# A hybrid decoder layer: first weights of down's second group split and stored during up, a cast moved behind bank copies, activation halves in two pieces

## The chip, the cores and the metric

The kernel runs on one core of a Trainium2 chip. The time is the device time of one execution in microseconds; before the change its median over three runs is 1188.48 us (1188.13 to 1190.49).

## The reference

One layer for 1024 prompt tokens and 64 decode tokens together (1088 columns), model width 1024, all in float32. A normalised input goes through one input projection into two mixers (retention with 8 heads, and sliding-window attention with 8 query heads), an output projection and a residual. Then comes the part of this case:

```python
hf = rms_norm(h, norm_ffn_gain)
h = h + jnp.square(jax.nn.relu(hf @ w_up)) @ w_down    # w_up: 1024 x 4096, w_down: 4096 x 1024
```

## The kernel before

Float32 products are made of three matmuls: each operand is split into a high half (a cast to float32r on ScalarE) and a low half (the operand minus the high half, on VectorE), and `mm3` multiplies high by high, low by high and high by low. `halve` (lines 791 and 792) is that cast and that subtraction. `wsplit` does it for one 128x512 piece of weights, in a buffer `wa` or `wb` of which there are four each.

Both big products of the MLP use Strassen's scheme with seven products of sums of quarter matrices. `left` is a generator that loads the raw weights of one tile (two loads of 512 KB, on ScalarE's DMA queue), forms the sums on GpSimd (POOL, lines 1046) and yields the split weights product by product. The order of the products is `PROD` for up and `DOWN = (1, 6, 7, 4, 5, 3, 2)` for down. Product one of a tile takes the quarter `a11` itself, the first 512 columns of the raw tile.

Up has 16 tiles, the calls `up(fp)`, of some 21 us each. A tile's squared activations, and their sums for Strassen's right side, are stored to DRAM (`u_d`) in four stores on SyncE's queue, three quarters first (line 1153) and four sums later (line 1173). After up, the pools of its operands are closed and `dn` takes their space.

Down has five groups of tiles: 2, 4, 4, 4 and 2 files of `w_down` (group index `g` = 0 to 4; files 0-1, 2-5, 6-9, 10-13, 14-15). For each group the seven products run in the order of `DOWN`. A product has eight units, (m, s) with m below 4 and s below 2; a unit accumulates over the group's files into one PSUM bank, three matmuls of 128x272 for each file. There are eight banks. Products 1, 5 and 2 start new sums, the others add on to what stands in the banks. After each unit the bank goes to an accumulator `a` in SBUF: the first time by a copy on ScalarE (line 1264, the last one of a product is kept in `copied[i]`), later by an addition on VectorE (line 1267). So a bank is not written by the next product before its copy or addition is done. The activations of a product are loaded from `u_d` (line 1246; for the first group's products seven, four and five at line 1221) and halved into `uh` and `ul`, two files at a time.

The order on each engine is set by a scheduler that simulates the program when it is built. `tc.issue_after(ins)` adds by hand that what is issued inside it on `ins`'s own engine stands behind `ins` in that engine's queue; other engines are not held. For the first product of groups 1 and 2 such ties hold ScalarE's weight loads (and casts) behind copies of the first group:

```python
behind = copied[(6, 6, 7, 4)[f] if g == 1 else 4] if g in (1, 2) and i == 1 else None
with tc.issue_after(behind) if behind else ExitStack():
    ws.append(next(gen))
```

Of the kernel before, what the change touches and what calls it, by code (L numbers as in the profile page):

```python
# [11 lines left out]
F32 = mybir.dt.float32  # L12
F32R = mybir.dt.float32r
AF = mybir.ActivationFunctionType
ALU = mybir.AluOpType
# [5 lines left out]
P = 128  # L21
# [15 lines left out]
def hymba_layer(ctx: ExitStack, tc: tile.TileContext, a: dict, o: dict):  # L37
    nc = tc.nc
# [10 lines left out]
    scratch = ctx.enter_context(tc.tile_pool(name="scratch", bufs=1, space=DRAM))  # L49
# [79 lines left out]
    ms_hi_d = scratch.tile([P, 4, T], F32, name="ms_hi_d")  # L129
    ms_lo_d = scratch.tile([P, 4, T], F32, name="ms_lo_d")  # L130
    y_d = scratch.tile([P, 4, 4, 2, Q], F32, name="y_d")
    u_d = [scratch.tile([P, 2, 2, 7, Q], F32, name=f"u_d{g}") for g in range(8)]

    def rsqrt_inplace(ap, n):
# [171 lines left out]
    w = wload(a["w_in"][2], 8, "wkv", "v")  # L306
    for t in range(9):
        off, c, r0 = tok_tile(t)
# [200 lines left out]
    for blk in range(4):  # L509
        w = wload(a["w_in"][3 + blk], 8, f"wqk{blk}")  # L510
# [9 lines left out]
    for blk in range(2):  # L520
        w = wload(a["w_in"][7 + blk], 8, f"wg{blk}")
# [264 lines left out]
    def pool(name, bufs=1, side=None, space=None):  # L786
        kw = {"space": space} if space else {}
        return tc.tile_pool(name=name, bufs=bufs, side=side, reuse_waits="tile", **kw)

    def halve(hi, lo, src, lo_eng):  # L790
        nc.scalar.copy(hi, src)  # L791
        lo_eng.tensor_tensor(lo, src, hi.bitcast(F32), ALU.subtract)  # L792

    def wsplit(src, tag, name, lo_eng):
        w = (mid if tag == "wb" else mw).tile([P, 2, 512], F32R, tag=tag, name=name, bufs=4)
        halve(w[:, 0, :], w[:, 1, :], src, lo_eng)
        return w
# [170 lines left out]
    mw = ctx.enter_context(pool("mw", side="right"))  # L968
# [54 lines left out]
    opx = ExitStack()  # L1023
# [9 lines left out]
                for x in "hl"  # L1033
            ]

    def left(order, src, name, lo_eng, raw_tag="raw", raw_pool=None, s_tag="S", s_pool=None, tags=("wa", "wb"), raws=None, sums=None):

        r1, r2 = raws or (
            rawload(src[:, i * 1024 : i * 1024 + 1024], f"{name}_r{i + 1}", raw_tag, raw_pool) for i in range(2)
        )  # L1040
        a11, a12, a21, a22 = r1[:, :512], r1[:, 512:], r2[:, :512], r2[:, 512:]
        have = {1: a11, 2: a12, 4: a22, **(sums or {})}

        def comb(i, p_, q_, op):
            t_ = have[i] = (s_pool or mid).tile([P, 512], F32, tag=s_tag, name=f"{name}_s{i}", bufs=10 if s_tag == "Sb" else 4)
            nc.gpsimd.tensor_tensor(t_, p_, q_, op)

        for n, i in enumerate(order):
            if i in (5, 6) and 5 not in have:
                comb(5, a21, a22, ALU.add)  # L1050
                comb(6, have[5], a11, ALU.subtract)
            if i == 7:
                comb(7, a11, a21, ALU.subtract)
            if i == 3:
                comb(3, a12, have[6], ALU.subtract)
            yield wsplit(have[i], tags[n % len(tags)], f"{name}_w{i}", lo_eng)

    late = lambda: bank("pso")
# [9 lines left out]
    for ms in ((0, 1), (2, 3), (4, 5), (6, 7)):  # L1068
# [3 lines left out]
        if ms == (6, 7):  # L1072
# [6 lines left out]
                sums={5: s56[:, :512], 6: s56[:, 512:]})  # L1079
# [13 lines left out]
    ux = ExitStack()  # L1093
    um = ux.enter_context(pool("u", side="right"))

    last_sub = {}

    def up(fp):
        gen = chain(ready, gen0) if fp == 0 else left(
            PROD, a["w_up"][fp], f"wu{fp}", nc.vector, tags=("wa", "wa", "wb", "wb"))  # L1100
        x, y, z = ([bank(f"ps{n}{s}") for s in range(2)] for n in "xyz")
        home = {1: (x, True), 2: (y, True), 6: (x, False), 5: (z, True), 7: (x, False), 4: (x, False), 3: (z, False)}
        ra, rb = ([um.tile([P, n, Q], F32, tag=f"r{n}{s}", name=f"r{n}t{fp}_{s}") for s in range(2)] for n in (3, 4))
        held, wait, ws = {}, [], {}
        order = [(i, s) for i in PROD for s in range(2)]
        if fp == 0:

            order = [(1, 0), (1, 1), (2, 0), (6, 0), (5, 0)] + [(i, 1) for i in (2, 6, 5)] + order[8:]

        def tq(n, s):  # L1110
            return um.tile([P, Q], F32, tag="tq", name=f"{n}{fp}_{s}", bufs=9)

        def add(n, s, bank_):
            t_ = held[n, s]
            nc.vector.tensor_tensor(t_, t_, bank_, ALU.add)
            return t_

        def act(t_, src, s, h, dst):

            nc.vector.scalar_tensor_tensor(t_, src, 0.0, rsf[:, s, h, :], ALU.max, ALU.mult)  # L1120
            return nc.scalar.activation(dst, t_, AF.Square)

        for i, s in order:
            if i not in ws:
                behind = last_sub[0, 0] if (fp, i) in ((1, 3), (2, 6)) else None
                with tc.issue_after(behind) if behind else ExitStack():
                    ws[i] = next(gen)
            w = ws[i]
            bk, first = home[i][0][s], home[i][1]
            for k in range(4):  # L1130
                lh, ll = (w[:, j, k * 128 : k * 128 + 128] for j in range(2))
                rh, rl = (ops[RIGHT[i]][s][j][:, k, :] for j in range(2))
                mm = mm3(bk, lh, ll, rh, rl, first and k == 0, k == 3, not first)
            if i in (1, 6, 7):
                t_ = held[i, s] = tq(f"m{i}", s)
                nc.scalar.copy(t_, bk)  # L1136
            if i == 2:
                t_ = add(1, s, bk)
                wait.append((t_, t_, s, 0, ra[s][:, B11, :]))
                if fp or s == 0:  # L1140
                    act(*wait.pop())
            if fp == 0 and (i, s) == (5, 0):
                norm(1)
            if fp == 0 and (i, s) == (5, 1):
                norm_spread(1, mm)
            if i == 7:
                if wait:
                    act(*wait.pop())
                t_ = add(7, s, z[s])
                act(t_, t_, s, 1, ra[s][:, B22, :])  # L1150
            if i == 4:
                squared = act(tq("v", s), bk, s, 0, ra[s][:, B21, :])
                nc.sync.dma_start(u_d[fp // 2][:, fp % 2, s, :3, :], ra[s])
            if fp == 15 and s == 1 and i == 2:
                first_down(1, ("1h", "1l", "2h", "2l"))()
            if fp == 15 and s == 1 and i == 5:
                split6.append(first_down(6, ("6h", "6l", "5h", "5l")))
            if i == 3:
                t_ = add(6, s, bk)
                if fp == 15 and s:  # L1160
                    with tc.issue_after(squared.ins):
                        split6[0]()
                r12 = um.tile([P, Q], F32, tag="r12", name=f"r12{fp}_{s}", bufs=2)
                act(t_, t_, s, 1, r12)
                b11, b21, b22 = (ra[s][:, i_, :] for i_ in (B11, B21, B22))
                t1, t2, t3, t4 = (rb[s][:, i_, :] for i_ in range(4))
                eng = nc.vector if fp in (0, 15) and s else nc.gpsimd
                sub = lambda o_, p_, q_: eng.tensor_tensor(o_, p_, q_, ALU.subtract)
                sub(t1, r12, b11)
                sub(t2, b22, t1)  # L1170
                last_sub[fp, s] = sub(t4, b21, t2).ins
                sub(t3, b22, r12)
                nc.sync.dma_start(u_d[fp // 2][:, fp % 2, s, 3:, :], rb[s])

    begun, raws1, sums1 = {}, [], {}

# [19 lines left out]
        return lambda: halve(u_hi, u_lo, u_raw, nc.vector)  # L1196

    split6 = []
    for fp in range(16):
        up(fp)  # L1200
    opx.close()
    ux.close()

# [19 lines left out]
    for g, (f0, nf) in enumerate(((0, 2), (2, 4), (6, 4), (10, 4), (14, 2))):  # L1223
        gens = []
        for f in range(nf):
            own = ("rawb", dn, "Sb", dn) if f else ("raw", mw, "S", mid)
            gens.append(left(
                DOWN, a["w_down"][f0 + f], f"wd{f0 + f}", nc.vector, *own, tags=("wb" if f % 2 else "wa",),
                raws=raws1 if (g, f) == (0, 1) else None, sums=sums1 if (g, f) == (0, 1) else None))
        banks = {}  # L1230
        for i in DOWN:
            ws = []
            for f, gen in enumerate(gens):
                behind = copied[(6, 6, 7, 4)[f] if g == 1 else 4] if g in (1, 2) and i == 1 else None
                with tc.issue_after(behind) if behind else ExitStack():
                    ws.append(next(gen))
            if g == 0 and i in begun:
# [6 lines left out]
            for f in () if g == 0 and i in begun else range(0, nf, 2):  # L1244
                if g or i in (3, 2):
                    nc.sync.dma_start(ur[:, f : f + 2], u_d[(f0 + f) // 2][:, :, :, RIGHT[i], :])
                with tc.issue_after(copied[{4: 6, 5: 7}[i]]) if g == 0 and i in (4, 5) else ExitStack():
                    halve(uu[0][:, f : f + 2], uu[1][:, f : f + 2], ur[:, f : f + 2], nc.vector)
            q_ = INTO[i]
            if q_ not in accs:  # L1250
                accs[q_] = dn.tile([P, 4, 2, Q], F32, tag=f"a{q_}", name=f"a{q_}")
# [147 lines left out]
```

## Time and profile before

| | us |
|---|---|
| median of three runs | 1188.48 |
| profiled execution, its own time | 1188.43 |
| its span | 1186.7 |
| TensorE busy in the span (PE) | 1169.6 |
| VectorE (DVE) | 839.1 |
| ScalarE (ACT) | 513.8 |
| GpSimd (POOL) | 494.2 |

PE is the matmuls and PEld the weight loads that overlap them; POOL is GpSimd, DVE VectorE, ACT ScalarE, SPq and ACTq the queues on which SyncE and ScalarE issue transfers. L792 is line 792. `out<-in` gives the tiles written and read. In a timeline the row's first two numbers are start and duration in us from the start of the span; the bracket is the idle time of the engine ahead of the instruction and what ended it. In a row of transfers the last number is the median time in us from issue to landing. Up ends and down begins around 840 us; the granted clock is 1.00 throughout.

### The profile page before, as it was taken

How to read it: one execution, taken by the hardware profiler on the slowest of the kernel's cores; microseconds unless marked ns; L12 is line 12 of the kernel's file. 1: busy time of each engine (PE TensorE's matmuls, PEld its weight loads, DVE VectorE, ACT ScalarE, POOL GpSimd, SP SyncE). 2: the span in 40 equal slices, each digit the busy share in tenths (PEclk: the TensorE clock that was granted, in tenths of full speed). 3: DMA queues.
4: the chain of work that ended last, by engine and by line, in shares of the span. 5: the costliest groups of instructions: out<-in, count | busy, mean ns of one | idle time of the engine just before them, and what ended most of it. 6: DMA issues, size and time to landing. Idle time of an engine off the chain costs nothing.

```text
span 1186.7 us, 23488 instructions
## 1 busy us (share of the span) xinstructions
PE 1169.6 (99%) x9405; PEld 1123.5 (95%) x9405; DVE 839.1 (71%) x1546; ACT 513.8 (43%) x1055; POOL 494.2 (42%) x393
## 2 busy tenths in 40 slices
PE   8999999999999999999999999999999999999998
PEld 7999988989778899999999999999989999999998
DVE  7556868632257769887766667666788787888676
ACT  8343544553334347644444444444642333333231
POOL 0125333332255542467666666566383142053000
PEclk9999999999999999999999999999999999999999
DMA  7221235333525555343444434444685456443225
GB/s 247 73 62 68 93 102 166 104 115 98 180 74 168 181 183 156 113 156 133 141 151 148 144 130 141 151 148 157 236 290 157 148 169 203 143 155 104 76 59 187
DMA packets 102277, 169.44 MB, mean 143 GB/s; under 512 B 12000, under 2 KB 68256, under 8 KB 101912
## 3 DMA queue, kind: packets, MB, share of 16 engines
q1 hardware_dynamic: 88807, 123.80, 31.5%
q10 hardware_dynamic: 10800, 35.23, 9.3%
q0 software_dynamic: 2560, 8.91, 2.3%
q8 instruction: 74, 1.21, 0.4%
q14 instruction: 36, 0.29, 0.1%
HBM read 114.30 MB, written 53.61 MB: 142 GB/s over the span
## 4 chain that ended last, share of the span: by engine, by line
PE 81%; DVE 6%; DMA 5%; issue 3%; ACT 2%; POOL 2%; SPq 0%; ACTq 0%; DVEq 0%; POOLq 0%
PE psd L176 9%; PE psd L177 9%; PE psd L175 9%; PE psx L175 5%; PE psx L177 5%; PE psx L176 5%; PE psz L175 2%; PE psz L177 2%; PE psz L176 2%; PE pst L175 2%; PE pst L176 2%; PE pst L177 2%; PE psf L175 2%; PE psf L177 2%; PE psf L176 2%
## 5 line engine op out<-in xcount | busy, mean ns | idle before, releaser
L175 PE MATMUL psd<-uh,wd_w 128*128 128x272 f32 x896 | 258.4, 288 | 3.2 <-DVE a L1267 2.4
L176 PE MATMUL psd<-uh,wd_w 128*128 128x272 f32 x896 | 259.3, 289 | 0.0
L177 PE MATMUL psd<-ul,wd_w 128*128 128x272 f32 x896 | 257.9, 288 | 0.7 <-DVE ul L792 0.7
L175 PEld LDWEIGHTS psd<-uh,wd_w 128*128 128x128 f32 x896 | 169.1, 189 | 4.3 <-DVE a L1267 3.4
L177 PEld LDWEIGHTS psd<-ul,wd_w 128*128 128x128 f32 x896 | 168.7, 188 | 0.9 <-DVE ul L792 0.9
L176 PEld LDWEIGHTS psd<-uh,wd_w 128*128 128x128 f32 x896 | 168.4, 188 | 0.0
L1267 DVE TENSOR_TENSOR a<-a,psd 128x272 f32<-128x272 f32 x248 | 101.9, 432 | 48.9 <-PE psd L177 48.8
L792 DVE TENSOR_TENSOR wu_w<-wu_s,wu_w 128x512 fp32r<-128x512 f32 x64 | 61.9, 971 | 49.8 <-ACT wu_w L791 49.2
L791 ACT CAST wd_w<-wd_s 128x512 fp32r<-128x512 f32 x64 | 37.5, 621 | 119.0 <-PE psd L177 107.2
L792 DVE TENSOR_TENSOR ul<-ur,uh 128x1088 fp32r<-128x1088 f32 x56 | 84.0, 1527 | 4.1 <-ACT uh L791 4.1
L1120 DVE SCALAR_TENSOR_TENSOR m<-m,rsf 128x272 f32<-128x272 f32 x96 | 72.9, 760 | 3.2 <-ACT rsf L914 0.5
L175 PE MATMUL psx<-op_1h,wu_w 128*128 128x272 f32 x256 | 74.3, 290 | 0.4 <-ACT m L1136 0.4
L177 PE MATMUL psx<-op_1l,wu_w 128*128 128x272 f32 x256 | 74.1, 289 | 0.0
L175 PE MATMUL psx<-op_0h,wu_w 128*128 128x272 f32 x256 | 74.1, 290 | 0.0
L177 PE MATMUL psx<-op_0l,wu_w 128*128 128x272 f32 x256 | 74.1, 289 | 0.0
L176 PE MATMUL psx<-op_1h,wu_w 128*128 128x272 f32 x256 | 73.7, 288 | 0.0
L176 PE MATMUL psx<-op_0h,wu_w 128*128 128x272 f32 x256 | 73.7, 288 | 0.0
L365 POOL TENSOR_TENSOR sp<-sp,ssp 128x1024 f32<-128x1024 f32 (+1 forms) x16 | 28.6, 1787 | 88.4 <-DVE ssp L364 60.1
L791 ACT CAST uh<-ur 128x1088 fp32r<-128x1088 f32 x56 | 59.7, 1101 | 12.7 <-PE psd L176 9.1
L175 PE MATMUL psf<-hnh,wqk_hi 128*128 128x384 f32 (+1 forms) x192 | 63.5, 331 | 0.2 <-DVE qkst L517 0.2
L177 PE MATMUL psf<-hnl,wqk_hi 128*128 128x384 f32 (+1 forms) x192 | 63.2, 329 | 0.0
L176 PE MATMUL psf<-hnh,wqk_lo 128*128 128x384 f32 (+1 forms) x192 | 62.8, 327 | 0.0
(343 smaller groups left out, 3619.4 us busy)
## 6 DMA issues: line engine op xcount, KB each, us to landing
ur<-u_d SPq DMA_DIRECT2D x53, 544.0 KB, 5.2
u_d<-r4t SPq DMA_DIRECT2D x32, 544.0 KB, 4.6
wu_r<-in_w_up ACTq DMA_DIRECT2D x32, 512.0 KB, 4.4
wd_r<-in_w_down ACTq DMA_DIRECT2D x30, 512.0 KB, 6.5
u_d<-r3t SPq DMA_DIRECT2D x32, 408.0 KB, 2.9
y<-in_xY POOLq DMA_DIRECT2D x16, 272.0 KB, 3.5
y_d<-y POOLq DMA_DIRECT2D x16, 272.0 KB, 3.2
yt<-y_d SPq DMA_DIRECT2D x16, 272.0 KB, 2.9
```

The costliest lines, as they stand in the source:

```text
L175: nc.tensor.matmul(ps, lh, rh, start=first, stop=False, skip_group_check=more)
L176: nc.tensor.matmul(ps, ll, rh, start=False, stop=False, skip_group_check=more)
L177: return nc.tensor.matmul(ps, lh, rl, start=False, stop=last, skip_group_check=more)
L365: nc.gpsimd.tensor_tensor(s, s, ss.unsqueeze(2).broadcast_to([P, 4, n]), ALU.mult)
L791: nc.scalar.copy(hi, src)
L792: lo_eng.tensor_tensor(lo, src, hi.bitcast(F32), ALU.subtract)
L1120: nc.vector.scalar_tensor_tensor(t_, src, 0.0, rsf[:, s, h, :], ALU.max, ALU.mult)
L1267: added[i] = nc.vector.tensor_tensor(to, to, ps, ALU.add).ins
```

## The change

Four edits.

- During up, after each of the tiles `fp` = 3 to 10, `split_down` takes half of a first quarter `a11` of files 2 to 5 (128x256): a load on SyncE's queue, tied behind the last store of that tile of up, a cast on ScalarE, a subtraction on VectorE, and a store of both halves to `wd_d` in DRAM. A new pool `pre` with one buffer holds the piece; it is closed with up's operands.
- In down's group 1, the first product's weights of the four files are loaded ready split from `wd_d` (512 KB each, SyncE's queue) instead of being cast and subtracted there. The raw loads stay, for the sums need them.
- In group 0 the weight casts of product five stand behind `copied[6]`, the last bank copy of product six.
- In group 0 the activations of product seven are halved file by file instead of two files at once.

```diff
+    wd_d = {f: scratch.tile([P, 2, 512], F32, name=f"wd_d{f}") for f in range(2, 6)}
...
+            if i == 1 and stored is not None:
+                w = (mid if tags[0] == "wb" else mw).tile([P, 2, 512], F32R, tag=tags[0], name=f"{name}_w1", bufs=4)
+                nc.sync.dma_start(w.bitcast(F32), stored)
+                yield w
+                continue
             yield wsplit(have[i], tags[n % len(tags)], f"{name}_w{i}", lo_eng)
...
-                nc.sync.dma_start(u_d[fp // 2][:, fp % 2, s, 3:, :], rb[s])
+                last_store[0] = nc.sync.dma_start(u_d[fp // 2][:, fp % 2, s, 3:, :], rb[s]).ins
...
+    pre = opx.enter_context(pool("pre", side="left"))
+
+    def split_down(f, c):
+        w = pre.tile([P, 2, 256], F32R, tag="pw", name=f"pw{f}_{c}")
+        with tc.issue_after(last_store[0]):
+            nc.sync.dma_start(w[:, 1, :].bitcast(F32), a["w_down"][f][:, c : c + 256])
+        nc.scalar.copy(w[:, 0, :], w[:, 1, :].bitcast(F32))
+        nc.vector.tensor_tensor(w[:, 1, :], w[:, 1, :].bitcast(F32), w[:, 0, :].bitcast(F32), ALU.subtract)
+        nc.sync.dma_start(wd_d[f][:, :, c : c + 256], w.bitcast(F32))
+
     for fp in range(16):
         up(fp)
+        if 2 < fp < 11:
+            split_down(2 + (fp - 3) // 2, 256 * ((fp - 3) % 2))
...
-                raws=raws1 if (g, f) == (0, 1) else None, sums=sums1 if (g, f) == (0, 1) else None))
+                raws=raws1 if (g, f) == (0, 1) else None, sums=sums1 if (g, f) == (0, 1) else None,
+                stored=wd_d[f0 + f] if g == 1 else None))
...
+                if (g, i) == (0, 5):
+                    behind = copied[6]
...
-                    halve(uu[0][:, f : f + 2], uu[1][:, f : f + 2], ur[:, f : f + 2], nc.vector)
+                    n = 1 if (g, i) == (0, 7) else 2
+                    for j in range(f, f + 2, n):
+                        halve(uu[0][:, j : j + n], uu[1][:, j : j + n], ur[:, j : j + n], nc.vector)
```

More of the change, by code (lines that the diff above doesn't have):

```diff
@@ L1034, in operand_tiles, with left @@
             ]
-    def left(order, src, name, lo_eng, raw_tag="raw", raw_pool=None, s_tag="S", s_pool=None, tags=("wa", "wb"), raws=None, sums=None):
+    def left(order, src, name, lo_eng, raw_tag="raw", raw_pool=None, s_tag="S", s_pool=None, tags=("wa", "wb"), raws=None, sums=None, stored=None):
         r1, r2 = raws or (
@@ L1094, in hymba_layer @@
     um = ux.enter_context(pool("u", side="right"))
-    last_sub = {}
+    last_sub, last_store = {}, [None]
     def up(fp):
```

## The prediction

> **What bounds the kernel now.** I read the page first, then the busy times by stage, then the waits of the weight loads (PEld) in order of time, and last the engines around each of those waits.
>
> ```profile
> span 1186.7 us, 23488 instructions
> PE 1169.6 (99%) x9405; PEld 1123.5 (95%) x9405; DVE 839.1 (71%) x1546; ACT 513.8 (43%) x1055; POOL 494.2 (42%) x393
> 500.00:838.00 338.00, 336.67 (x2712) 336.06 (x2712) 239.03 (x353) 151.11 (x344) 214.31 (x186) 1.00 0.43 145
> 848.00:866.00 18.00, 17.35 (x138) 17.14 (x137) 11.73 (x12) 14.45 (x34) 5.73 (x5) 1.00 1.04 384
> 872.00:878.00 6.00, 5.88 (x47) 5.66 (x46) 6.00 (x10) 2.85 (x5) 5.84 (x5) 1.00 0.98 333
> 878.00:884.00 6.00, 3.62 (x24) 2.96 (x24) 6.00 (x9) 0.46 (x1) 6.00 (x4) 1.00 0.74 233
> 900.00:1000.00 100.00, 100.00 (x797) 100.00 (x796) 81.48 (x126) 35.49 (x51) 26.89 (x18) 1.00 0.51 163
> ```
>
> The columns are the stretch, its length, and the busy time of PE, PEld, DVE, ACT, POOL. TensorE is the bound nearly everywhere, so only its holes are for sale. Up (500 to 838) has 1.3 us of them in 338. Down from its second group on has none: 100.00 of 100 us, 797 matmuls, 0.125 us each. The holes lie where down's first group ends: in 878 to 884 PE is busy 3.62 of 6 us while DVE is busy all 6. The weight loads show each hole:
>
> ```profile
> 845.82 0.19 PEld L175 LDWEIGHTS psd<-uh,wd_w 128*128 128x128 f32 x1 [0.96 <-ACT a L1264]
> 853.16 0.19 PEld L177 LDWEIGHTS psd<-ul,wd_w 128*128 128x128 f32 x1 [0.85 <-DVE ul L792]
> 874.31 0.19 PEld L175 LDWEIGHTS psd<-uh,wd_w 128*128 128x128 f32 x1 [0.34 <-DVE a L1267]
> 879.55 0.19 PEld L175 LDWEIGHTS psd<-uh,wd_w 128*128 128x128 f32 x1 [1.41 <-DVE a L1267]
> 881.84 0.19 PEld L175 LDWEIGHTS psd<-uh,wd_w 128*128 128x128 f32 x1 [0.74 <-DVE a L1267]
> 883.52 0.19 PEld L175 LDWEIGHTS psd<-uh,wd_w 128*128 128x128 f32 x1 [0.88 <-DVE a L1267]
> ```
>
> Six waits, 5.18 us: one on a bank copy of ScalarE, one on the low half of product seven's activations, four (3.37 us) on DVE's bank additions. That is all the change can win in down. After 883.52 the last 24 matmuls of product two remain, so group two starts at 883.5 + 24 x 0.125 = 886.5.
>
> **Part 1: the cast behind bank copies.** The engines at the first two waits:
>
> ```profile
> 844.79 0.62 ACT L791 CAST wd_w<-wd_s 128x512 fp32r<-128x512 f32 x1 [1.42 <-PE psd L177]
> 844.81 0.53 ACTq L1221 DMA_DIRECT2D ur<-u_d  x1
> 845.38 2.41 ACT L1264 COPY a<-psd 128x272 f32<-128x272 f32 x8
> 850.68 1.10 ACT L791 CAST uh<-ur 128x1088 fp32r<-128x1088 f32 x1 [1.05 <-DMA ur<-u_d]
> 851.82 1.29 DVE L792 TENSOR_TENSOR ul<-ur,uh 128x1088 fp32r<-128x1088 f32 x1 [1.15 <-ACT uh L791]
> 867.36 1.11 ACT L791 CAST uh<-ur 128x1088 fp32r<-128x1088 f32 x1 [1.94 <-DMA ur<-u_d]
> ```
>
> A weight cast stands ahead of product one's eight copies. It waits 1.42 us for TensorE to end product one (its buffer was product one's weights, so it is product five's cast), runs 0.62 us, and then the copies begin at 845.38; TensorE, due for the first copied bank, has lost 0.96. The edit puts both casts of product five behind product six's last copy. The copies can then start where ScalarE went idle, 844.79 - 1.42 = 843.4, two us earlier, and I count the whole 0.96 (bounds: 0 if another cast takes the place, 0.96). The casts cost nothing where they go: product five starts two products of 48 x 0.125 = 6 us after six, against 2 x 0.62 us of casts and 1.29 of DVE or less. Cover gone, they would cost 1.24 on ScalarE ahead of product four's activations.
>
> **Part 2: halves in product seven.** TensorE waits 0.85 for a low half that is late because its load was issued at 844.81, behind that same cast, and landed at 850.68. Two things help. The load is no longer behind a cast that waits for TensorE: up to 1.4 us earlier. And cast and subtraction go in two pieces, so the first file's halves are ready about half of 1.10 + 1.29 = 1.2 us earlier, for two more instructions with some fixed time each. But TensorE arrives 0.96 earlier too. I take 0.6 of the 0.85 (bounds 0 and 0.85).
>
> **Part 3: four stored weights in group two.**
>
> ```profile
> 865.45 0.89 DVE L792 TENSOR_TENSOR wd_w<-wd_r,wd_w 128x512 fp32r<-128x512 f32 x1 [0.81 <-ACT wd_w L791]
> 872.48 1.43 DVE L792 TENSOR_TENSOR wd_w<-wd_r,wd_w 128x512 fp32r<-128x512 f32 x1
> 875.23 1.62 DVE L792 TENSOR_TENSOR wd_w<-wd_r,wd_w 128x512 fp32r<-128x512 f32 x1
> 877.12 2.03 DVE L792 TENSOR_TENSOR ul<-ur,uh 128x1088 fp32r<-128x1088 f32 x1
> 881.71 1.41 DVE L792 TENSOR_TENSOR wd_w<-wd_r,wd_w 128x512 fp32r<-128x512 f32 x1
> 886.32 0.68 DVE L792 TENSOR_TENSOR wd_w<-wd_s,wd_w 128x512 fp32r<-128x512 f32 x1
> 877.96 6.30 POOL L1046 TENSOR_TENSOR wd_s<-wd_r,wd_r 128x512 f32<-128x512 f32 x3
> ```
>
> The four subtractions go: 0.89 + 1.43 + 1.62 + 1.41 = 5.35 us of a DVE that is full, each stretched beside POOL (0.68 where POOL is idle, 886.32). Four casts of 0.62 go from ScalarE. The first subtraction bought nothing, since DVE then sat waiting for the activations that ScalarE casts at 867.36; the other three are 4.46 us ahead of waits of 3.37. What is late next is DVE still: additions and activation halves fill most of 866 to 884, and TensorE comes 1.6 us sooner. So I leave a remainder.
>
> The price is four loads of 512 KB on SyncE's queue, each waiting for a weight buffer: two till product four ends, two till product five ends. Behind them on that queue stand only activation loads of product one and six of group two. The scheduler may set the former ahead. ScalarE's queue keeps the eight raw loads behind its copies. The transfer engines are full then (shares 1.04 and 0.98 above):
>
> ```profile
> 862.97 1.23 SPq L1246 DMA_DIRECT2D ur<-u_d  x2
> 868.70 1.30 ACTq L806 DMA_DIRECT2D wd_r<-in_w_down  x3
> 870.03 0.94 ACTq L806 DMA_DIRECT2D wd_r<-in_w_down  x2
> wd_r<-in_w_down ACTq DMA_DIRECT2D x1, 512.0 KB, 9.7
> 872.23 1.71 SPq L1246 DMA_DIRECT2D ur<-u_d  x2
> ur<-u_d SPq DMA_DIRECT2D x1, 544.0 KB, 9.3
> ```
>
> The last of five raw loads (issued 870.6, 9.7 us) landed at 880.3; the activation load issued at 872.2 landed at 881.5, behind all five: near the order of issue. At 384 GB/s a 0.524 MB load is 1.37 us of the engines, so 5.5 us are added. All holes gone, group two starts at 881.3 and takes its third and fourth file's weights after 6 and 9 matmuls, 882.1 and 882.4. Those two loads are issued when product five ends, two products of 6 us before 881.3, about 869, among the five raws. Two raws ahead: the last lands near 880.3 + 5.5 - 3 x 1.37 = 881.7, in time. All five ahead: 885.8, 3.4 late. I take two or three ahead, and with DVE's remainder leave 0.7 of the 3.37: a gain of 2.7 (bounds 0 and 3.37).
>
> The Trainium skill ("DMA: Bandwidth & Descriptors", Queues, rings and completion order) says that each transfer engine goes round-robin between the queues, a packet at a time. By it the two late loads alternate with the raws, one or two raws ahead of each, and the last lands at 881.7: in time, and the 2.7 would be 3.0 or more. The 9.3 us row does not agree with it, since that load, issued 1.6 us after the last raw, waited for all five; so rival B keeps its place.
>
> **Part 4: the price in up.** Eight tiles each get a 128 KB load, a cast and a subtraction of 128x256, and a 256 KB store:
>
> ```profile
> L791 ACT CAST op_1h<-f 128x272 fp32r<-128x272 f32 x6 | 2.1, 412 | 2.2 <-DVE f L890 2.2
> L792 DVE TENSOR_TENSOR op_1l<-f,op_1h 128x272 fp32r<-128x272 f32 x8 | 3.1, 440 | 0.4 <-ACT op_1h L791 0.4
> PE psz L176 <- DVE wu_w L792: 0.9, 1, 0.9
> ACT r3t L1121 <- POOL r4t L1168: 29.8, 28, 3.0
> SPq L1153 <- ACT r3t L1121: 215.6, 32, 52.4
> yt<-y_d SPq DMA_DIRECT2D x16, 272.0 KB, 2.9
> ```
>
> By the 128x272 rows a tile pays 0.41 us on ScalarE and 0.44 on DVE (twice that beside POOL), in 21 us of which 45% and 71% are used. SyncE's tie puts the load behind the tile's last store. Behind it and the new store stand the next tile's stores, whose queue idles for 215.6 us in all, so it delays nobody. A cast that stands early in ScalarE's queue holds the copies behind it for a load's 2.9 us at most; ScalarE waits up to 3.0 us for POOL today, 28 times, and TensorE waited for one 0.9 in the stage. Between 0 and 8 x (0.41 + 0.88) = 10.3 us, I take 0.2, near the idle end. The new buffer closes before down, so it holds no one.
>
> **The sum.** -0.96 - 0.6 - 2.7 + 0.2 = -4.1. The profiled execution took 1188.43 us (span 1186.7 and 1.7 around it), 0.05 under the median of 1188.48; I forecast **1184.4**.
>
> **Rivals.**
> A, the forecast: 1184.4, own range 1182.9 to 1186.0.
> B, the stored weights land late: all five raws ahead, the fourth file's at 885.8 instead of 882.4. Group two then gains 1.9 instead of 5.2: 1188.43 - 1.9 + 0.2 = 1186.7; if product one's activations stand behind them on SyncE too, near 1188. For it: full engines, the landing order. Against: two of the four are issued 4 us before the raws.
> C, DVE stays the bound: the order of its queue, not its load, makes the four waits. Only parts 1 and 2 pay: 1188.43 - 1.56 + 0.2 = 1187.1. For it: DVE busy 12 of 12 us from 872 to 884. Against: 5.35 us leave it.
> D, slower: up loses a hole in each of the eight tiles, the cast or subtraction standing in its queue ahead of the copies and additions TensorE waits for while its load is still on the way. It decides from (4.3 + 2.4) / 8 = 0.8 us a tile; at 1.0 us the time is 1184.2 + 8 = 1192.2. Against: the waits of 3.0 us that TensorE did not feel. For it: a sequence new to every queue.
> The Trainium skill ("GPSIMD Engine Reference", Specifications) says that POOL shares its SBUF interfaces with DVE instructions of two SBUF inputs; the subtraction is one. The trace agrees (1.41 beside POOL, 0.68 alone).
>
> **How the numbers follow.** A 0.60, B 0.14, C 0.12, D 0.14. This kernel's measurement tells about 0.2% (2.4 us) from no change. A is faster; B and C lie within 0.2%, a fifth of them past it: faster 0.65, same 0.21, slower 0.14. The range runs from every hole gone (5.18, and 0.06 more for each of the six, since a weight load lasts 0.19 where the beat is 0.125: 1188.43 - 5.5 = 1182.9) to the start of D, 1189.2.
>
> **What would show it.** Right: no wait for a bank copy near 845; no wait over 0.4 for a low half near 851; waits for additions between 866 and 884 under 1 us in sum; group two starting near 882.3; stored loads landed before it; up as full as now. Wrong: a wait of group two's first product for a transfer; TensorE holes in the eight tiles; DVE still full with the same four waits.

## The result and the profile after

Over 19 runs each the median went from 1188.99 to 1186.45 us; the ratio is 0.9978, 95% interval 0.9971 to 0.9985: about 2.6 us faster, where 4.1 had been forecast. The profiled execution took 1186.29 us. The changed file has more lines, so line numbers move: 1267 is 1290, 1264 is 1287, 792 is 793, 791 is 792, 1246 is 1267.

The page, and busy times by stage (columns as in the prediction), of the changed kernel:

```profile
span 1184.4 us, 23548 instructions
PE 1168.4 (99%) x9405; PEld 1123.3 (95%) x9405; DVE 832.2 (70%) x1551; ACT 512.0 (43%) x1060; POOL 489.6 (41%) x393
500.00:838.00 338.00, 334.63 (x2692) 333.67 (x2691) 231.92 (x357) 150.04 (x350) 212.62 (x186) 1.00 0.45 154
872.00:878.00 6.00, 5.64 (x45) 5.42 (x45) 6.00 (x11) 2.11 (x2) 2.65 (x2) 1.00 1.02 403
878.00:884.00 6.00, 6.00 (x50) 6.00 (x49) 6.00 (x12) 1.14 (x2) 5.52 (x4) 1.00 1.07 383
900.00:1000.00 100.00, 100.00 (x797) 100.00 (x796) 80.63 (x125) 33.51 (x48) 26.72 (x18) 1.00 0.53 170
```

The hole at the end of group one is filled: in 878 to 884 TensorE is busy 6.00 us, before 3.62. VectorE is busy all of the time from 872 to 884, as before: TensorE now comes sooner and VectorE's other work has moved up, so its busy share alone would not have told that the waits went. But up lost what it had not lost before, 334.63 busy of 338 against 336.67; from 560 on, with the eight tiles, it is 276.15 of 278 against 278.00. The weight loads show where, from tile 3 of up to the end of down's first group:

```profile
601.90 0.19 PEld L176 LDWEIGHTS psx<-op_0h,wu_w 128*128 128x128 f32 x1 [1.22 <-ACT m L1142]
666.58 0.19 PEld L176 LDWEIGHTS psx<-op_0h,wu_w 128*128 128x128 f32 x1 [1.06 <-ACT m L1142]
871.09 0.19 PEld L176 LDWEIGHTS psd<-uh,wd_w 128*128 128x128 f32 x1 [0.99 <-ACT a L1287]
873.98 0.19 PEld L176 LDWEIGHTS psd<-uh,wd_w 128*128 128x128 f32 x1 [0.58 <-DVE a L1290]
```

In down 5.2 us of waits became 1.6; in up two new ones of 2.3 us stand behind ScalarE's copy of a bank (line 1142). SyncE's loads and ScalarE's casts of the pieces, in tile 3 with the first hole and in tile 4 without one:

```profile
594.05 0.38 SPq L1210 DMA_DIRECT2D pw<-in_w_down  x1
601.16 0.40 ACT L1211 CAST pw<-pw 128x256 fp32r<-128x256 f32 x1 [4.14 <-DMA pw<-in_w_down]
601.47 0.67 ACT L1142 COPY m<-psx 128x272 f32<-128x272 f32 x2
617.11 0.38 SPq L1210 DMA_DIRECT2D pw<-in_w_down  x1
621.49 0.41 ACT L1211 CAST pw<-pw 128x256 fp32r<-128x256 f32 x1 [2.02 <-DMA pw<-in_w_down]
pw<-in_w_down SPq DMA_DIRECT2D x1, 128.0 KB, 7.1
pw<-in_w_down SPq DMA_DIRECT2D x1, 128.0 KB, 4.4
  DMA pw<-in_w_down: 21.9, 8
DMA to landing us min/median/max: 4.3/5.6/7.1
```

The two rows of loads are those of 594.05 and 617.11; the last two rows count all eight. The cast is the first in the queue, the load takes 4.3 to 7.1 us, and two copies that TensorE needs stand behind it. ScalarE idles 21.9 us for these loads in the eight tiles. The landings of 7.1 us (tile 3) and 6.4 (tile 6) gave the two holes; the six of 5.8 or less gave none.

### The profile page after: what moved, and what is told of

Read it like the earlier page. It is cut to its first block, busy times and chain, and to the rows that moved or that the text cites. A ratio compares the mean times of both kernels' runs of the same rounds, so it can differ in the third digit from the quotient of the medians.

```text
span 1184.4 us, 23548 instructions
## 1 busy us (share of the span) xinstructions
PE 1168.4 (99%) x9405; PEld 1123.3 (95%) x9405; DVE 832.2 (70%) x1551; ACT 512.0 (43%) x1060; POOL 489.6 (41%) x393
## 4 chain that ended last, share of the span: by engine, by line
PE 78%; DVE 6%; DMA 6%; POOL 4%; issue 3%; ACT 2%; SPq 0%; POOLq 0%; DVEq 0%; ACTq 0%
PE psd L177 9%; PE psd L176 9%; PE psd L178 9%; PE psx L176 4%; PE psx L178 4%; PE psx L177 4%; PE pst L176 2%; PE pst L177 2%; PE pst L178 2%; PE psz L176 2%; PE psz L178 2%; PE psz L177 2%; PE psf L176 2%; PE psf L178 2%; PE psf L177 2%
## 5 line engine op out<-in xcount | busy, mean ns | idle before, releaser
L793 DVE TENSOR_TENSOR wu_w<-wu_s,wu_w 128x512 fp32r<-128x512 f32 x64 | 55.3, 868 | 51.0 <-ACT wu_w L792 50.7
L793 DVE TENSOR_TENSOR ul<-ur,uh 128x1088 fp32r<-128x1088 f32 (+1 forms) x57 | 83.7, 1496 | 6.3 <-ACT uh L792 6.3
L1126 DVE SCALAR_TENSOR_TENSOR m<-m,rsf 128x272 f32<-128x272 f32 x96 | 68.8, 717 | 3.2 <-ACT rsf L915 0.5
L792 ACT CAST uh<-ur 128x1088 fp32r<-128x1088 f32 (+1 forms) x57 | 59.7, 1085 | 15.0 <-PE psd L177 10.1
```

## The experiments

Each row of waits below is for TensorE's weight loads from 560 to 900 us of the span, that is the eight tiles and down's first group: what was waited for, then us in total, times, longest. Each profile is one execution. Before the change there are the six waits of the prediction: 3.4 in four behind additions, 1.0 behind a copy, 0.9 for a low half, 5.2 us in sum.

**The work in up alone.** Nothing reads the stored pieces.

```diff
-                stored=wd_d[f0 + f] if g == 1 else None))
+                stored=None))
-                if (g, i) == (0, 5):
-                    behind = copied[6]
-                    n = 1 if (g, i) == (0, 7) else 2
+                    n = 2
```

> Only the work in up: the eight pieces are loaded, split and stored, and nothing reads them; down is as before. Theory 1 (a queue in order): the piece's cast stands in ScalarE's queue ahead of TensorE's bank copies while its load is still on the way, so up shows one to three new holes of about 1.2 us, each behind a copy that follows a piece's cast; down keeps its six waits of 5.2 us; 1.5 to 3.5 us slower than before. Rival (the holes in up are the chance of one execution, the pieces are free as in the prediction): no new hole, within 0.3 us of before.

```profile
PEld psd L176 <- DVE a L1288: 4.0, 4, 1.5
PEld psd L176 <- ACT a L1285: 1.9, 2, 1.0
PEld psx L176 <- ACT m L1142: 1.0, 1, 1.0
```

Ratio 1.0008 (0.9996 to 1.0019). A hole behind a bank copy in up is there again, in tile 3, so it belongs to this work; its price in time, 0.9 us, is below what theory 1 expected and its interval takes in no change, so it is the trace and not the time that speaks against the rival. The waits in down did not stay as they were: product seven's is gone without any edit to it, a second wait for a copy has come, and those behind additions are 4.0 instead of 3.4.

**One piece split, eight stores.** The stored weights of the four files are then not those that group two needs; down's work is the same.

```diff
+        if not kept_w:
             w = pre.tile([P, 2, 256], F32R, tag="pw", name=f"pw{f}_{c}")
...
+            kept_w.append(w)
+        with tc.issue_after(last_store[0]):
+            nc.sync.dma_start(wd_d[f][:, :, c : c + 256], kept_w[0].bitcast(F32))
```

> All of the change, but only one piece is loaded and split, and this one piece is stored eight times, once per tile (so down's stored weights are wrong numbers). Theory 1: seven of the eight casts that wait for a load are gone, so at most one hole is left in up; 1.2 to 2.4 us faster than the change. Rival (it is the transfers of the pieces, not the waiting cast): the eight stores stay, so the holes stay, and the time is the change's.

```profile
PEld psd L176 <- ACT a L1292: 1.8, 1, 1.8
PEld psx L176 <- ACT m L1142: 0.2, 1, 0.2
PEld psd L176 <- DVE a L1295: 0.2, 1, 0.2
```

Ratio 0.9965 (0.9953 to 0.9978), about 1.5 us better than the change as theory 1 had it, though the two intervals overlap. The hole at the one cast left is 0.2 us; at the seven tiles with a store alone there is none. Seven loads and subtractions went with the casts, so this run does not yet tell the waiting cast from the work; the next one does.

**The late cast.** The load stays; the cast, and with it the subtraction and the store, goes one tile later.

```diff
-        nc.scalar.copy(w[:, 0, :], w[:, 1, :].bitcast(F32))
+        with tc.issue_after(last_square[0]):      # product four of the next tile of up
+            nc.scalar.copy(w[:, 0, :], w[:, 1, :].bitcast(F32))
```

> The change, with the piece loaded where it was but cast one tile of up later, tied on ScalarE behind the squares of product four of that tile (some 15 us after the load's issue, against 4 to 7 us of landing). Theory 1 (a cast that waits in the queue for its load): ScalarE waits for no piece, no hole of over 0.3 us in tiles 3 to 11, up as long as before the change, down's first group as in the change: 1 to 2.4 us faster than the change, 0.9960 to 0.9975 of before. Rival (the extra 0.4 us on ScalarE and 0.9 on VectorE a tile are what is late): the holes stay in number and size, only elsewhere in the tile.

```profile
PEld psd L176 <- DVE a L1297: 0.8, 1, 0.8
PEld psd L176 <- ACT a L1294: 0.7, 1, 0.7
606.57 0.40 ACT L1216 CAST pw<-pw 128x256 fp32r<-128x256 f32 x1
```

Same eight loads, casts and subtractions, no wait ahead of the cast, no hole in up: 0.9966 (0.9953 to 0.9978). Run once more beside the change on the same chip:

> The late cast in up alone, once more beside the change on the same chip. Theory 1: 1 to 2.4 us below the change. Rival: the change and it within 0.5 us, the earlier difference being the scatter of the executions.

> The change itself, for the comparison with the late cast: 0.997 to 0.9985 of before, with one or two holes of about 1.2 us in up's tiles 4 to 11 and under 2 us of holes in down's first group.

The late cast, again without a hole in up, gave 0.9963 (0.9949 to 0.9976), the change 0.9978 (0.9968 to 0.9988), medians 1184.81 and 1186.06. The change's waits this time:

```profile
PEld psd L176 <- DVE a L1290: 1.1, 1, 1.1
PEld psd L176 <- ACT a L1287: 0.5, 1, 0.5
PEld psx L176 <- ACT m L1142: 0.5, 2, 0.3
```

So the holes in up swing between 0.5 and 2.3 us from one execution to the next, with the landing of the loads (the latest took 7.1 us in the first profile and 6.1 in this one), and the late cast ends that: all five profiles here with eight early casts show a hole behind a bank copy in up, the four with late casts show none. The difference in time, 1.3 to 1.8 us, is at the lower end of what was expected; the two intervals overlap, and it is the traces that carry the verdict.

**The parts in down, one by one.** Cast and halves without the stored weights:

> Only the cast behind bank copies and the halves in product seven; no stored weights, nothing new in up. Theory 2 (the two waits add to the others): the waits of 0.96 and 0.85 at products six and seven go, the four behind VectorE's additions stay at 3.4; 1.8 us faster than before. Rival (VectorE is the bound from product five on): the two waits go, those behind additions grow by as much, group two starts at the same time after up, no gain.

```profile
PEld psd L176 <- DVE a L1288: 3.5, 4, 1.4
PEld psd L176 <- ACT a L1285: 0.6, 1, 0.6
```

Ratio 0.9992 (0.9982 to 1.0002). The waits at products six and seven are gone, those behind additions stay at 3.5 and do not grow, as theory 2 had it; a new one of 0.6 takes a part of the 1.8 back. The time alone fits theory 2's 1.8 us and the rival's nothing equally. The cast alone:

> Only the cast behind bank copies. Theory: product six's wait of 0.96 goes, and product seven's of 0.85 goes or falls under 0.3 because its load is issued earlier, once the cast no longer stands ahead of it. Rival: product seven's load is issued when it was, at its space's release, so its wait stays, or grows by what TensorE comes earlier, to 1.0 to 1.9.

```profile
PEld psd L176 <- DVE a L1288: 3.3, 4, 1.4
PEld psd L176 <- ACT a L1285: 0.7, 1, 0.7
843.80 0.43 ACT L1127 ACTIVATE r<-m 128x272 f32<-128x272 f32 x1 [1.71 <-DVE m L1126]
843.82 0.53 ACTq L1237 DMA_DIRECT2D ur<-u_d  x1
```

Before, the same activation and the load's row of the prediction (844.81) stand further apart:

```profile
842.94 0.43 ACT L1121 ACTIVATE r<-m 128x272 f32<-128x272 f32 x1 [1.71 <-DVE m L1120]
```

Ratio 0.9990 (0.9981 to 0.9998), and product seven's wait is gone too. With the cast out of the way the load of product seven's activations is issued 0.02 us after up's last activation starts, before 1.87 us after it, so the rival (issued when it was) is out. It also landed 4.0 us after its issue instead of 5.8. A sooner landing is enough by itself: where the cast is not tied, the load took 5.4 us with the stored weights alone (wait 0.4) and 5.0 with only the work in up (no wait). The halves alone:

> Only the halves in product seven. Theory: product six's wait of 0.96 stays, product seven's 0.85 falls under 0.3: 0.6 us at most, which the time can't show. Rival: the load's landing is what is late, and 0.5 or more stays.

```profile
PEld psd L176 <- DVE a L1286: 4.0, 4, 1.5
PEld psd L176 <- ACT a L1283: 2.0, 2, 1.1
```

Ratio 1.0000 (0.9991 to 1.0009). Product seven's wait is gone, as the theory had it, but product four's copy now costs 1.1 and the additions 4.0: what was won at product seven is lost further on. The load landed in 4.7 us here, less than the 5.0 that needed no halves, so no run shows that the halves win anything; beside the cast they have nothing left to win. The stored weights without cast and halves:

> Only the stored weights, with their work in up; the cast of product five and product seven's halves are as before. Theory 2: the first two waits stay at 1.8, the four behind additions shrink from 3.4 to under 1.5, up loses 1.5 to 3.5: within 1.5 us of before. Rival (VectorE's relief is larger where TensorE comes later): the waits behind additions go to nothing, and down's first group gains all of 3.4, so the time is 0 to 2 us below before and as good as the change.

```profile
PEld psd L176 <- ACT a L1285: 1.7, 2, 1.0
PEld psx L176 <- ACT m L1142: 1.3, 2, 1.1
PEld psd L176 <- DVE a L1288: 0.6, 1, 0.6
PEld psd L178 <- DVE ul L793: 0.4, 1, 0.4
```

Ratio 0.9980 (0.9968 to 0.9992): as good as the whole change, which is the rival's outcome, though the interval (1.0 to 3.8 us) reaches into theory 2's. The waits are theory 2's: those behind additions fell from 3.4 to 0.6, not to nothing, product six's stayed at 0.96, and product seven's went to 0.4 with its load's landing. The sum of waits is 1.3 us below before. The stored weights alone reach the change's gain; what the cast adds to them, the time did not show.

**The wait that comes next.** In all of these runs a bank copy makes TensorE wait near 870 (874 with the work in up alone). In the change:

```profile
868.16 1.11 ACT L792 CAST uh<-ur 128x1088 fp32r<-128x1088 f32 x1 [3.46 <-PE psd L178]
869.66 1.10 ACT L792 CAST uh<-ur 128x1088 fp32r<-128x1088 f32 x1 [0.39 <-DMA ur<-u_d]
870.66 0.38 ACT L1287 COPY a<-psd 128x272 f32<-128x272 f32 x1
```

It is product four's last copy, and the two activation casts ahead of it wait for their loads. (The first row's bracket names TensorE, but the load, issued at 856.51, took 11.6 us and landed at 868.1.) Before, the same copy ended just as TensorE came. A first try, on top of the late cast, tied product three's cast behind product four's last copy, and product two's subtraction behind the last addition of product five:

```diff
+                held_by = {..., 3: copied.get(4), 2: added.get(5)}.get(i) if g == 0 else None
```

> As the one before, and in down's first group product three's activation casts are tied behind the last bank copy of product four, and product two's subtraction behind the last addition of product five. Theory 3 (the two holes left in down's first group, 1.05 behind a bank copy that stands behind two casts waiting for their load, and 0.64 behind an addition that stands behind a subtraction, are orders of a queue too): both go or fall under 0.5 us in sum, another 1.2 us. Rival (full transfer engines are what is late there): the holes stay at the activations themselves, at the first matmuls of products three and two, and nothing is gained.

```profile
PEld psd L176 <- ACT a L1295: 1.7, 1, 1.7
868.81 1.10 ACT L792 CAST uh<-ur 128x1088 fp32r<-128x1088 f32 x1 [5.71 <-PE psd L178]
869.81 0.38 ACT L1295 COPY a<-psd 128x272 f32<-128x272 f32 x1
```

Missed: a cast still stands ahead of the copy, for product two's was not held on ScalarE, and the hole stays: 1.7, where the runs without this tie have 0.5 to 1.8. Two waits of 0.6 and 0.2 for activation halves came behind it. Ratio 0.9980 (0.9970 to 0.9990). With both casts held (and the subtraction free), also on top of the late cast:

```diff
-                with tc.issue_after(copied[{4: 6, 5: 7}[i]]) if g == 0 and i in (4, 5) else ExitStack():
+                with tc.issue_after(copied[{4: 6, 5: 7, 3: 4, 2: 4}[i]]) if g == 0 and i in (4, 5, 3, 2) else ExitStack():
```

> The late cast in up, and the activation casts of products three and two both tied behind the last bank copy of product four (the run before tied only product three's, and product two's cast went ahead of that copy in its place). Theory 3: the last copy of product four runs near 864, as soon as its bank is done, not near 870, and the hole of 0.8 to 1.8 us at product five's last unit goes; the addition's hole of 0.6 to 0.9 stays; 0.8 to 1 us below the late cast alone, which the time can just show. Rival (the transfer engines are late there whatever the order): TensorE stands as long a microsecond later, at product three's first matmuls, for its activations.

```profile
PEld psd L176 <- DVE a L1297: 0.6, 1, 0.6
PEld psd L176 <- issue: 0.4, 1, 0.4
PEld psd L178 <- DVE ul L793: 0.4, 1, 0.4
866.69 1.10 ACT L792 CAST uh<-ur 128x1088 fp32r<-128x1088 f32 x1 [2.90 <-DMA ur<-u_d]
```

The copy's wait is gone. A smaller one, 0.4 us at product three's low half, takes part of it back: there the rival is right, the load is late. (The 0.4 under "issue" lies in group two, at 894.81, and the profile names no cause.) Ratio 0.9954 (0.9941 to 0.9966), median 1183.66: the best version here, ahead of before and of the change. It is 1.1 us below the late cast alone, as theory 3 had it, but the intervals overlap: the wait's end is shown by the trace, its worth in time is not.

**The late loads.** In the change the third and fourth file's stored weights are issued at 876.8 and 877.3 and landed 9.8 and 10.6 us later, at 886.6 and 887.9. That is 5 us after product five ended (871.8, six matmuls after its last wait): product six's activation loads for group two went out ahead of them on SyncE's queue, at 873.61, and the profile puts the last 1.9 us down to the landing of a raw load. Group two starts at 884.5 and would, unit by unit, need the third file after 6 matmuls, at 885.3; yet nobody waits. The program's order shows why: the scheduler, when it built the changed kernel, put the first two files' matmuls of all eight units (48, 6 us) ahead of the third's. The last run takes that order away:

```diff
+                        with tc.issue_after(unit_end[0]) if (g, i) == (1, 1) and unit_end[0] else ExitStack():
+                            mm = mm3(ps, lh, ll, ...)
+                    unit_end[0] = mm.ins
```

> The change, with TensorE's matmuls of group two's first product tied unit by unit (all four files of a unit before the next unit). In the change the scheduler has put the first two files' matmuls of all eight units ahead, so the third file's weights are needed 6 us after the start and not 0.8. Theory 4 (the stored weights of the third and fourth file land late, as rival B of the prediction has it, and only that order hides it): they land at 886 to 888 of the span again, TensorE waits for them 1 to 3 us in the first unit, and the time is as much above the change. Rival (the loads follow what is asked of them: needed earlier, they are issued and land earlier): no wait for a transfer there, the time of the change.

```profile
886.32 0.19 PEld L176 LDWEIGHTS psd<-uh,wd_w 128*128 128x128 f32 x1 [1.41 <-ACT wd_w L792]
887.55 0.19 PEld L176 LDWEIGHTS psd<-uh,wd_w 128*128 128x128 f32 x1 [0.80 <-DMA wd_w<-wd_d]
876.80 0.88 SPq L1059 DMA_DIRECT2D wd_w<-wd_d  x2
888.00:891.00 3.00, 3.00 (x15) 3.00 (x15) 3.00 (x2) 0.00 (x0) 2.92 (x2) 0.50 0.25 81
```

Ratio 0.9998 (0.9989 to 1.0008): all of the change's gain is lost. The loads are issued when they were, and TensorE waits twice for them (the first row names a cast of ScalarE, which had long been done; the third file's load was the last to come), 2.2 us in sum, and then runs 3 us at half its clock. The rival (needed earlier, issued earlier) is out. Its wait for the copy near 870 (1.8) and its holes in up (1.4) are no larger than in other runs with early casts.

## Why the prediction was right or wrong

- **Direction, bound and range: right.** The holes at the end of group one were what was for sale, and down after 900 stayed full, as forecast. The median, 1186.45, lies inside the wide range but just above the forecast's own (1182.9 to 1186.0) and near rival B's 1186.7; against the before of its own 19 runs the gain is 2.6 us. The range's upper end, 1189.2, is called the start of D, which by D's own figures (2.4 us over 1188.43) would be 1190.8; nothing hangs on it.
- **Part 1: right, and larger than its name.** Its 0.96 is gone in every run that has the cast tied, and stands at 0.96 in each of the three that have not. In the tied runs product seven's wait went with it, for its load is issued 1.85 us sooner after up's last activation. How much of that wait was there to win is chance: untied, it was 0.9, 0.4 or nothing as the load landed in 5.8, 5.4 or 5.0 us.
- **Part 2: oversized.** It was given 0.6; alone it measured 1.0000, and with the cast there is nothing left for it. The parts were added up as if each wait ended by itself; a wait won at product seven came back behind product four's copy and the additions.
- **Part 3: near in size, wrong in its reason, and spared by luck.** 3.37 us were to shrink to 0.7; they shrank to 0.6 behind additions and 1.0 behind the copy of product four, which the prediction did not name as next. Rival C is excluded: the four waits fell when the four subtractions (and their casts) went, and did not when only product five's casts were moved. Rival B's late loads came true, and worse than it said (887.9 against 885.8): the issue near 869 was wrong, it came at 876.8, and so was "two or three ahead", for all five raw loads had been issued by 872. The two queues did not alternate load by load either, by which the last would have landed at 881.7 (figures in the last section). The late loads did not cost, for a reason that no step had: the build reordered TensorE's matmuls. Without that the ratio is 0.9998, and no gain is left, less than the 1.7 us that B had left over.
- **Part 4: the step that failed.** It took 0.2 "near the idle end", where the change's profile has 2.3 us and the second one 0.5. It had named the mechanism, as rival D: the cast that stands early holds the copies. It went wrong on the load: "2.9 us at most" was the median of a 272 KB load elsewhere, while the piece's 128 KB load, issued right behind two stores of 544 KB on the same queue, took 4.3 to 7.1. And that TensorE had not felt waits of 3.0 us said nothing about waits of 4.1, ahead of other copies.
- **The sum.** Down's waits fell by 3.6 (4.3 forecast), up took 0.5 to 2.3 back (0.2 forecast): 1.3 to 3.1, beside 2.6 measured. That the forecast came as near as it did owes something to the order of the matmuls, which it had not counted on.

## What to carry to other kernels

A piece of work slipped into a full stage is priced by what stands behind it in its engine's queue while its operand is on the way, and not by its own 0.4 us; its load is to be priced in the queue and the stretch it will run in, not by a median from elsewhere. The cure is to tie the consumer behind something that surely comes after the landing: the same work one tile later cost no hole. And when a wait is removed, look for the next instruction that ended just in time in the trace of before (the copy at 870): it is the next wait.

## What the runs showed of the hardware

- In the run with the order taken away, after waits of 1.41 and 0.80 us close together, the granted clock fell to 0.50 and 15 matmuls took 3 us, 0.20 us each instead of 0.125; by that the half clock cost about 1.5 us on top of the waits, an estimate. Holes of 1.2 us that stood alone cost no clock. What decides it these runs do not show, and the share of idle time does not: TensorE was busy 2.20 of 4 us there (884 to 888), and before the change 2.29 of 4 us (878 to 882) at 1.00. The Trainium skill ("TensorE: Matmul & The Clock Gate", Part 1) says that the gate goes to half rate after an idle window of some 3.4 us; here half rate came though TensorE worked about half of the time before it, so the trace agrees with the half rate, not with a fully idle window.
- A load's time to land can't be read off its size: 4.3 to 7.1 us for 128 KB in up, behind two stores on its queue, against the 2.9 of 272 KB loads elsewhere; 8.4 to 10.6 for 512 KB at the end of group one, where the transfer engines were full (share 1.02 and 1.07). That the stores ahead are the reason in up is likely, but no run moved the load.
- Where both queues had loads out, one at a time had nearly all of the transfer engines. Before the change ScalarE's queue (q10 in the rows of queues) had a share of 0.94 from 871 to 876 and SyncE's (q1) 0.007, though a load of SyncE's had been issued at 872.2. In the change SyncE's queue had all from 868 to 872 while ScalarE's raw loads were issued from 869.7, and ScalarE's had 0.92 from 874 to 878 while SyncE's activation and stored loads were issued; from 882 to 887 SyncE's had all again. That is the time in which the third and fourth stored weights landed.
